# A hybrid attention and Fourier layer on eight cores: the Fourier projection on half the tokens, own keys computed late, side work spread over attention

## The chip, the cores and the metric

The kernel runs on all eight cores of one Trainium2 chip. Each pair of cores has one batch entry of four; each core owns 1024 of its 2048 tokens. Cores exchange nothing. The metric is the device time of the slowest core, in microseconds (us). Some runs are in a second, slower state, in which the cores of one die show a lower granted TensorE clock: in the run of 1853.86 us of the changed kernel cores 0 to 3 had 0.87 and took 1799 to 1852 us, cores 4 to 7 had 0.98 to 0.99 and took 1634 to 1638 us. A ratio is the mean time of one kernel's fast runs over that of the other's of the same rounds on the same chip, so it is not quite the ratio of the medians quoted beside it.

Names: PE is TensorE, ACT ScalarE, DVE VectorE, POOL GpSimd, SP SyncE. "ada blocks" are the 48 column blocks of the weight matrix that makes shift, scale and gate from the conditioning vector (tiles wada, wadm, wadb, by the buffer they land in).

## The reference, cut to what matters

```python
mod = silu(c) @ w_ada + b_ada                  # shift1, scale1, gate1, shift2, scale2, gate2
h = rmsnorm(x, g1) * (1 + scale1) + shift1
q, k, v, u = split(h @ w_in)                   # 1536 | 512 | 512 | 512 columns
q = rope(rmsnorm(q)); k = rope(rmsnorm(k))
attn = softmax(q @ [k_ctx, k].T / sqrt(128)) @ [v_ctx, v]     # 12 heads, 4 key heads, 256 context keys
four = Re(fft2(u over (positions, 128 channels))) @ w_f       # per group of 128 channels
x = x + gate1 * (concat(attn, four) @ w_out)
x = x + gate2 * (relu(modulate(rmsnorm(x, g2), ...) @ w1)**2 @ w2)
return rmsnorm(x, final_g)
```

A core needs keys and values for all 2048 tokens and 256 context tokens, but queries only for its own 1024. For the Fourier part it needs u of all positions.

Of the kernel before, what the change touches and what calls it, by code (L numbers as in the profile page):

```python
# [409 lines left out]
ORDER = [8, 12, 9, 13, 10, 14, 11, 15, 0, 4, 1, 5, 16, 17, 2, 6, 3, 7]  # L410
KORDER = [ORDER[n] for n in (5, 6, 7, 0, 8, 1, 9, 2, 10, 3, 11, 4, 14, 15, 16, 17)]

# [12 lines left out]
def _slots():  # L425
    o = 0
    for n, w in (('ident', 128), ('ones', 128), ('selb', 384), ('sel2', 2), ('dcol', 8)):
        CB[n] = (o, w)
        o += w
    CB['_'] = (o, 0)  # L430
    o = 0
    for n, w in (('g1', 16), ('g2', 16), ('fg', 16), ('bada', 96), ('c', 32), ('qg', 256), ('kg', 256), ('dmask', 1)):
        CF[n] = (o, w)
        o += w
    CF['_'] = (o, 0)
# [5 lines left out]
def build_program():  # L441
# [10 lines left out]
    wvu_d = din("w_vu", [128, 16 * 1024])  # L452
# [8 lines left out]
    ct_d = din("dft_c", [128, 8 * 512])  # L461
    st_d = din("dft_s", [128, 8 * 512])
    rr_d = din("dft_r", [2, 512])
# [3 lines left out]
    with ExitStack() as st:  # L467
# [22 lines left out]
        stat = small('stat', [18, 3])  # L490
# [3 lines left out]
        dsum = small('dsum', [4])  # L494
        dbf = small('dbf', [4], BF16)
# [3 lines left out]
        o_ub = o[0]  # L499
        ub = [small('ub_%d' % i, [512], BF16) for i in range(2)]  # L500
# [7 lines left out]
        ident, ones, sel2 = cbv('ident'), cbv('ones'), cbv('sel2')  # L508
# [7 lines left out]
        WVU = at('wvu', 60, [16, 1024], BF16)  # L516
        WV, WU = WVU[:, :, 0:512], WVU[:, :, 512:1024]
        WK = at('wk', 92, [16, 512], BF16)
        WQ = [at('wq_0', 60, [16, 512], BF16), at('wq_1', 44, [16, 512], BF16)]
        Ue = at('ue', 44, [8, 512], BF16)  # L520
        Uo = at('uo', 52, [8, 512], BF16)
        qT = at('qT', 76, [12, 1024], BF16)
        mixF = at('mixF', 100, [4, 1024], BF16)
# [5 lines left out]
        XS = [at('xs_%d' % i, kb, [16, 128]) for i, kb in enumerate((144, 152, 160, 192))]  # L529
        XI = [0, 1, 2, 3, 0, 1, 2, 0, 1, 2, 0, 1, 0, 1, 0, 1, 0, 1]  # L530
        SQ = [at('sqx_%d' % i, 168 + 4 * i, [16, 128], BF16) for i in range(2)]
        Y = [at('y_%d' % i, 176 + 2 * i, [512]) for i in range(4)]
        YL = Y[0:1] + [at('yl_%d' % i, kb, [512]) for i, kb in enumerate((46, 54, 140, 142, 186, 190))]
# [3 lines left out]
        BR = [at('br_%d' % i, 192 + i, [512], BF16) for i in range(2)]  # L537
        BK, BKC, BVD = [at(n, 194 + 2 * i, [512]) for i, n in enumerate(('bk', 'bkc', 'bvd'))]
        BQ = [at('bq_0', 194, [512]), at('bq_1', 196, [512])]
# [4 lines left out]
        CT = at('dftc', 144, [8, 512], BF16)  # L544
        ST = at('dfts', 152, [8, 512], BF16)
        AB = [at('ab_%d' % i, 160 + i, [512], BF16) for i in range(4)]
        WCS = at('wcs', 164, [3, 4, 128], BF16)
        RR = [at('rr_0', 167, [512], BF16), at('rr_1', 206, [512], BF16)]
        WFT = at('wft', 168, [512])
        CCS = at('ccs', 170, [256])  # L550
# [8 lines left out]
        SQA = R.buf('sqa', o_ub, [512])  # L559
# [27 lines left out]
        R.dma('sp', cf, cf_d[:, :], 'cf')  # L587
        R.dma('pool', cb, cb_d[:, :], 'cb')
# [6 lines left out]
        def ada(i, slots, key, dlevel, level, banks, after=()):  # L595
# [3 lines left out]
            d = R.dma('pool', w.rearrange("p k n -> p (k n)"), rows(wada_d, i), '%s%d' % (key, s), level=dlevel, after=after)  # L599
# [16 lines left out]
        def bias_rows(w, bank, level):  # L616

            R.level = level
            R.mms([(PS[bank][32 * j:32 * j + 32, :], shp[:, q + j, :], w[:, q + j, :], q == 0, q == 12)
                   for q in range(0, 16, 4) for j in range(4)])  # L620
            R.copy(BR[0], PS[bank])
            R.tt(BR[1], PS[bank], BR[0], ALU.subtract)

        def bias_bc(sel, bank, dst):
            R.mms([(PS[bank], sel, BR[0], True, False), (PS[bank], sel, BR[1], False, True)])
            R.copy(dst, PS[bank])
# [12 lines left out]

        last = []  # L640
        for i in range(8):
            last = ada(8 + i, AD0, 'ada', 0.0, 0.0, [7, 6], last)
            last = [R.dma('pool', WVU[:, 2 * i:2 * i + 2, :].rearrange("p k n -> p (k n)"),
                          wvu_d[:, 2048 * i:2048 * (i + 1)], 'wvu_%d' % i, level=0.0, after=last)]
# [54 lines left out]
        HS = [0, 1, 2, 3, 4, 5, 6, 7, 0, 1, 2, 3, 4, 5, 6, 7, 4, 5]  # L699
        hslot = {}  # L700
        NLATE = 7
        ny = 0

        def vu(n):
# [6 lines left out]
            sq = SQ[n % 2]  # L711
            R.act(sq.rearrange("p k n -> p (k n)"), x.rearrange("p k n -> p (k n)"), AF.Square)
            sb = 6 + n % 2 if n < 3 else 5
# [5 lines left out]
            h = H[HS[n]]  # L719
            hslot[t] = (h, rstd)  # L720
            w_ = 2 if n < 3 else 8
            R.level = 0.95
            for q in range(0, 16 if n < 3 else 8, w_):
                R.tt(h[:, q:q + w_, :], x[:, q:q + w_, :],
                     gs[:, q:q + w_, r].unsqueeze(2).to_broadcast([128, w_, 128]), ALU.mult)
            if n >= 3:
# [8 lines left out]
            b = proj(WV, n, 2) if n < 3 else proj(WV, rot('pb', 3))  # L735
# [5 lines left out]
            if r == 0:  # L741
                b = proj(WU, 3 + n, 2) if n < 3 else proj(WU, rot('pb', 3))
                j = (0 if t < 8 else 4) + t % 4
                if t % 8 < 4:
                    R.act(UA, PS[b], AF.Copy, scale=rstd)
                    R.ts(s3[:, 2:3], rstd, -1.0, None, ALU.mult)
                else:
                    R.ts(s3[:, 2:3], rstd, -1.0, None, ALU.mult)
                    R.stt(Ue[:, j, :], PS[b], rstd, UA, ALU.mult, ALU.add)
                    R.stt(Uo[:, j, :], PS[b], s3[:, 2:3], UA, ALU.mult, ALU.add)  # L750
                    if t % 4 == 0:
                        R.act(ub[t // 8][0:1, :], PS[b][0:1, :], AF.Copy, scale=rstd[0:1, :])

            def keys():
                R.level = 1
                b = proj(WK, 3 + (rot('kb', 2) if n < NLATE else 0))
                y = YL[n] if n < NLATE else Y[1 + rot('yk', 3)]
# [17 lines left out]
        first = [vu(n) for n in range(4)]  # L775
        last = load_win(3, WK, 'wk', 0.1, last)
        for i in range(8):
            last = ada(i, AD0[0:2], 'adz', 0.2, 0.5, [7, 6], last)
# [7 lines left out]

        chains = [keys() for keys in first] + [vu(n)() for n in range(4, NLATE)]
        some = [vu(n) for n in range(NLATE, 10)]
        for n in (5, 6):
            chains[n](0)  # L790
        for n in range(NLATE, 18):
            if n >= 15:
                some += [vu(i) for i in range(15, 18) if n == 15]
            (some.pop(0) if some else vu(n))()()
            if n < NLATE + 5:
                chains[n - NLATE]()
            if 10 <= n < 15:
                ada(6 + n, ADM, 'adm', 1, 1, [4], last)


        def q_block(cbk, pbanks, tbanks, tiles=range(8)):
            w = WQ[cbk % 2]
            bq = BQ[cbk % 2]
            if 0 in tiles:
                bias_rows(w, tbanks[rot('tq', len(tbanks))], R.level)
                bias_bc(selb[0], tbanks[rot('tq', len(tbanks))], bq)
            for t in tiles:
                h, rstd = hslot[t]
                b = pbanks[rot('pq', len(pbanks))]
                R.acc(PS[b], [(h[:, k, :], w[:, k, :]) for k in range(16)])  # L810
                yield qk(b, Y[rot('yd', 4)], rstd, bq, RQ[t // 4][:, t % 4, :], qg2, qT[:, cbk * 4:cbk * 4 + 4, t * 128:(t + 1) * 128])

        def load_wq(cbk, level):
            load_win(cbk, WQ[cbk % 2], 'wq%d' % (cbk % 2), level)


# [3 lines left out]
        for i in range(2):  # L820
            R.dma('pool', RR[i][0:1, :], rr_d[i:i + 1, :], 'rr%d' % i)
        for i in range(2):
            R.dma('sp', RQ[i].rearrange("p k n -> p (k n)"), ropeq_d[:, 512 * i:512 * (i + 1)], 'ropeq%d' % i)
# [3 lines left out]
        def mb():  # L827
            return 6 + rot('misc', 2)
        for i in range(2):
# [4 lines left out]
            if i == 1:  # L834
                R.ts(WCS[:, 2, :, :].rearrange("p g d -> p (g d)"), PS[b], -1.0, None, ALU.mult)
        b = mb()
        for g in range(4):
            R.mms([(PS[b][:, g:g + 1], Ue[:, j, g * 128:(g + 1) * 128], cb[:, CB['dcol'][0] + j:CB['dcol'][0] + j + 1], j == 0, j == 7)
                   for j in range(8)])
        R.copy(dsum, PS[b][:, 0:4])  # L840
        for g in range(4):
# [3 lines left out]
            R.acc(PS[b], [(Ue[:, j, gc], CT[:, j, :]) for j in range(8)] + [(ub[i][0:1, gc], RR[i][0:1, :]) for i in range(2)], step=5)  # L845
            R.copy(xb_, PS[b], 'act')
            R.tt(xb_[:, 0:1], PS[b][:, 0:1], buc[:, g:g + 1], ALU.add)
            R.tt(dbf[:, g:g + 1], PS[b][:, 0:1], dsum[:, g:g + 1], ALU.add)
            b = mb()
            R.acc(PS[b], [(Uo[:, j, gc], ST[:, j, :]) for j in range(8)])  # L850
# [5 lines left out]
            R.mms([(PS[b][:, 1:512], WCS[:, 0, g, :], xb_[:, 1:512], True, False),  # L856
# [8 lines left out]
        for out in q_block(0, [0, 1, 2, 3], [5], range(4)):  # L865
            if done:
                done(5)
# [326 lines left out]
```

## The kernel before: the parts that the change touches

A helper records every operation with what it reads and writes. A list scheduler then orders each engine's stream beforehand with modelled durations, by level and program order. Each engine gets its stream in that order, and the traces show it kept: the six cores whose traces hold all matmul records (10687) have them in one and the same order. Because of the helper all matmuls have the same line in the profile, and one goes by tile names.

A token tile n (128 tokens) is scaled into h. V and U projections follow (16 matmuls of 512 columns each), then K. The shift enters later as a bias (tile bk and others), since h W + shift W can be split:

```python
def vu(n):
    ...                                        # x tile loaded, sum of squares, h = x * gs
    b = proj(WV, ...)                          # V
    R.act(V[:, n, :, 0:128], h3(PS[b]), AF.Copy, scale=rstd)
    if r == 0:                                 # all 16 latent tiles
        b = proj(WU, ...)                      # U; tokens i and 2048 - i in paired tiles
        if t % 8 < 4: R.act(UA, PS[b], AF.Copy, scale=rstd)
        else:                                  # even and odd part of the pair
            R.stt(Ue[:, j, :], PS[b], rstd, UA, ALU.mult, ALU.add)
            R.stt(Uo[:, j, :], PS[b], s3[:, 2:3], UA, ALU.mult, ALU.add)
    def keys(): ...                            # K, and link(): bias, norm, rope, transpose into kT
```

The position DFT uses cosines on the even part and sines on the odd part, each over 8 tiles of 128 positions, for 4 channel groups:

```python
R.acc(PS[b], [(Ue[:, j, gc], CT[:, j, :]) for j in range(8)] + [(ub[i][0:1, gc], RR[i][0:1, :]) for i in range(2)], step=5)
R.acc(PS[b], [(Uo[:, j, gc], ST[:, j, :]) for j in range(8)])
```

Attention has 24 units (12 heads, two query halves), each with 18 key chunks: one 512-column score matmul, exp on ACT, four 129-column matmuls with V. Query projections ("side work") and ada blocks are handed out between the chunks.

## Time and profile before

Median 1669.6 us of 4 runs (1669.31 to 1721.56).

| what | number | view |
|---|---|---|
| span of the profiled core | 1668.6 us | page, first line |
| matmul work at full rate | 1538.9 us | my sum, below |
| shift bias bk ready | 199 us | chain of waits |
| first score matmul / last one | 341 / 651 us | timeline |
| longest unbroken piece of the MLP, 3921 matmuls | 842 us, 215 ns each | chain of waits |

"Matmul work at full rate" is a sum over all matmul records of columns / 2.4 GHz + 1.5 ns, at least 27 ns each, a quarter for the 32-column groups (in this trace four of these start within 10 ns, the next four 216 ns after the first). The constants are read from the starts of matmuls in this trace, from 300 us on: those of 512, 256 and 128 columns start 216, 109 and 56 ns apart (medians), which is 0.417 ns a column, or 2.4 GHz. The 1.5 ns come from the mean of 214.7 ns in the MLP. Those of one or two columns start 25 to 27 ns apart. "Lost" below is the length of a stage less this sum in it. This is needed because the busy share of PE says little: a matmul of 512 columns is shown as 379 ns long, while they start 215 ns apart.

Lines of the page, kernel before: the span, busy time and count of each engine, and two rows of slices (one digit per 1/40 of the span, in tenths: granted TensorE clock, and the DMA share):

```profile
span 1668.6 us, 28572 instructions; the slowest of 8 cores (1657.8 to 1668.6 us)
...
PE 1583.4 (95%) x10687; PEld 812.0 (49%) x10687; DVE 699.8 (42%) x1261; ACT 653.2 (39%) x1459; POOL 114.6 (7%) x182
...
PEclk9789999999999999999999999999999999999999
DMA  9999875288677995055253255424542454245206
```

The windows view by stage: length, then per engine busy us and instruction count, then granted clock, DMA share and GB/s. The limits are the end of the V loads, the shift, and the first and last score matmul:

```profile
core 1: us, PE busy (x) PEld busy (x) DVE busy (x) ACT busy (x) POOL busy (x), PEclk, DMA share, GB/s
0.00:98.00 98.00, 43.21 (x372) 18.85 (x372) 14.20 (x47) 12.63 (x18) 12.59 (x39) 0.80 1.00 186
98.00:199.00 101.00, 99.57 (x842) 49.97 (x842) 23.45 (x48) 57.39 (x130) 3.70 (x7) 0.97 0.98 221
199.00:341.00 142.00, 132.67 (x991) 65.53 (x990) 96.05 (x193) 88.60 (x345) 5.97 (x16) 0.98 0.47 97
341.00:560.00 219.00, 216.88 (x2398) 142.43 (x2397) 122.97 (x299) 156.45 (x338) 16.52 (x32) 1.00 0.81 140
560.00:651.00 91.00, 86.57 (x1148) 64.48 (x1146) 18.05 (x73) 81.69 (x165) 3.16 (x6) 0.98 0.90 179
```

In the first 98 us DMA is full (share 1.00) and the clock is low (0.80); afterwards PE is nearly always busy (99, 93, 99 and 95% of the next four rows). In the fifth row ACT is busy 82 of 91 us. PE's waits in the first 100 us of the kernel before, with what ended them (total us, times, longest), then, of the same kernel, four pieces of the chain that ended last (start, us, what):

```profile
PE ps L116 <- DMA wada_77<-w_ada: 23.7, 2, 22.9
PE ps L116 <- DMA wvu<-w_vu: 20.1, 8, 5.0
```

```profile
199.40 0.70 DVE bk L168
...
255.52 16.91 DMA wadm<-w_ada
...
562.30 43.41 DMA wadb_82<-w_ada
...
784.65 841.96 PE ps L116 x3921
```

The waits show that loads set PE's pace at the start. The chain shows where else something other than PE decided: the shift at 199 us, wadm in the key stage, and 43 us of wadb late in attention. Its last large piece is most of the MLP. Two groups of matmuls of the kernel before by form, for later (output and inputs, shapes, count, busy us and mean ns of one, idle time before): 64 V and U matmuls of one buffer, and the cosine half of the DFT:

```profile
L116 PE MATMUL ps<-wvu,h_62 128*128 128x512 bf16 x64 | 14.9, 379 | 0.0
...
L116 PE MATMUL ps<-dftc,ue 128*128 128x512 bf16 x32 | 7.6, 379 | 0.1
```

### The profile page before, as it was taken

To read this page: it belongs to the slowest core of one execution; us is meant where nothing else is said; L and a number is where in the kernel's file an instruction comes from. 1 tells how busy PE (TensorE), PEld (TensorE's weight loads), DVE (VectorE), ACT (ScalarE), POOL (GpSimd) and SP (SyncE) were. 2 spreads that over 40 slices of the span, in tenths; PEclk is the share of its full clock that TensorE was granted. 3 is DMA by queue.
4 is the path that set the end of the run, shared out by engine and by line. 5 is a ranking of instruction groups with operands and counts; after the bars stand their busy time and mean duration, and the time that the engine had idled before them with its cause. 6 is when DMAs were issued, how large, how long until landed. Compare 5 with 4: busy or idle time off the path is not lost.

```text
span 1668.6 us, 28572 instructions; the slowest of 8 cores (1657.8 to 1668.6 us)
## 1 busy us (share of the span) xinstructions
PE 1583.4 (95%) x10687; PEld 812.0 (49%) x10687; DVE 699.8 (42%) x1261; ACT 653.2 (39%) x1459; POOL 114.6 (7%) x182
## 2 busy tenths in 40 slices
PE   1689999999999999999999999999999999999996
PEld 0245544456666666444444444444444444444446
DVE  1122474765555312243444444444444444444236
ACT  1055586457777886145211111111111111111266
POOL 1100000000000000331000000000000000000032
PEclk9789999999999999999999999999999999999999
DMA  9999875288677995055253255424542454245206
GB/s 207 170 204 227 184 167 94 47 128 146 116 133 132 204 172 165 1 101 101 51 101 63 45 95 102 70 45 89 101 76 45 82 102 82 42 79 101 51 1 203
DMA packets 29669, 180.48 MB, mean 108 GB/s; under 512 B 2656, under 2 KB 10080, under 8 KB 13664
## 3 DMA queue, kind: packets, MB, share of 16 engines
q0 software_dynamic: 15472, 140.68, 47.7%
q1 hardware_dynamic: 14064, 37.97, 7.0%
q8 instruction: 89, 1.46, 0.3%
q14 instruction: 44, 0.36, 0.1%
HBM read 310.94 MB, written 8.39 MB: 191 GB/s over the span
## 4 chain that ended last, share of the span: by engine, by line
PE 83%; DMA 12%; ACT 2%; issue 1%; DVE 1%; POOL 0%; another core or an unknown queue 0%; DVEq 0%; ACTq 0%; POOLq 0%; SPq 0%
PE ps L116 83%; DMA wvu<-w_vu 5%; DMA wadb_82<-w_ada 3%; DMA wadm<-w_ada 2%; DMA wada_77<-w_ada 1%; DMA xs_86<-xt 1%; PE ps L128 1%; DMA wq_69<-w_in 1%; ACT h_2_150 L147 0%; ACT sqx_90 L147 0%; ACT h_64 L147 0%; ACT t_0_103 L147 0%; ACT h_63 L147 0%; ACT h_66 L147 0%; ACT sqx_89 L147 0%
## 5 line engine op out<-in xcount | busy, mean ns | idle before, releaser
L155 DVE SCALAR_TENSOR_TENSOR acc_147<-ps,modcol,acc_147 128x512 f32<-128x512 f32 (+2 forms) x288 | 197.4, 691 | 256.0 <-PE ps L116 238.9
L116 PE MATMUL ps<-a_1_160,w_1_158 128*128 128x512 bf16 (+2 forms) x1152 | 240.9, 355 | 0.0
L116 PE MATMUL ps<-a_0_159,w_0_157 128*128 128x512 bf16 (+2 forms) x1152 | 240.9, 355 | 0.0
L155 DVE SCALAR_TENSOR_TENSOR acc_145<-ps,modcol,acc_145 128x512 f32<-128x512 f32 x128 | 96.2, 751 | 176.6 <-PE ps L116 167.2
L116 PEld LDWEIGHTS ps<-a_0_159,w_0_157 128*128 128x128 bf16 x1152 | 108.5, 98 | 114.7
L116 PEld LDWEIGHTS ps<-a_1_160,w_1_158 128*128 128x128 bf16 x1152 | 108.7, 98 | 114.0
L155 DVE SCALAR_TENSOR_TENSOR acc_146<-ps,modcol,acc_146 128x512 f32<-128x512 f32 x128 | 96.2, 751 | 136.8 <-PE ps L116 127.4
L116 PE MATMUL ps<-qT,kT 128*128 128x512 bf16 x432 | 152.0, 380 | 1.0 <-ACT qst L147 0.5
L116 PE MATMUL ps<-h_0_148,w_0_155 128*128 128x512 bf16 x512 | 115.4, 379 | 0.0
L116 PE MATMUL ps<-h_0_148,w_1_156 128*128 128x512 bf16 x512 | 115.2, 379 | 0.0
L116 PE MATMUL ps<-h_2_150,w_0_155 128*128 128x512 bf16 x384 | 88.1, 379 | 0.3 <-ACT h_2_150 L147 0.3
L116 PE MATMUL ps<-h_2_150,w_1_156 128*128 128x512 bf16 x384 | 88.1, 379 | 0.0
L147 ACT ACTIVATE rs_164<-ps 128x512 f32<-128x512 f32 x32 | 19.1, 597 | 162.9 <-PE ps L116 162.9
L147 ACT ACTIVATE rs_161<-ps 128x512 f32<-128x512 f32 x32 | 19.1, 597 | 162.0 <-PE ps L116 162.0
L147 ACT ACTIVATE rs_163<-ps 128x512 f32<-128x512 f32 x32 | 19.1, 596 | 161.7 <-PE ps L116 161.7
L147 ACT ACTIVATE rs_162<-ps 128x512 f32<-128x512 f32 x32 | 19.1, 596 | 160.7 <-PE ps L116 160.7
L116 PEld LDWEIGHTS ps<-h_0_148,w_0_155 128*128 128x128 bf16 x512 | 50.2, 98 | 60.3
L116 PEld LDWEIGHTS ps<-h_0_148,w_1_156 128*128 128x128 bf16 x512 | 50.2, 98 | 60.3
L152 DVE TENSOR_TENSOR modcol<-ps,cf 128x4 f32<-128x4 f32 x48 | 7.6, 159 | 129.3 <-PE ps L116 129.3
L116 PEld LDWEIGHTS ps<-h_2_150,w_0_155 128*128 128x128 bf16 x384 | 37.4, 98 | 46.1 <-issue 1.2
L116 PEld LDWEIGHTS ps<-h_2_150,w_1_156 128*128 128x128 bf16 x384 | 37.5, 98 | 45.3
L116 PEld LDWEIGHTS ps<-qT,kT 128*128 128x128 bf16 x432 | 40.8, 97 | 17.1 <-issue 4.6
(432 smaller groups left out, 2374.1 us busy)
## 6 DMA issues: line engine op xcount, KB each, us to landing
w_0_155<-w POOLq DMA_DIRECT2D x8, 2048.0 KB, 16.1
w_0_157<-w POOLq DMA_DIRECT2D x8, 2048.0 KB, 23.1
w_1_156<-w POOLq DMA_DIRECT2D x8, 2048.0 KB, 16.3
w_1_158<-w POOLq DMA_DIRECT2D x8, 2048.0 KB, 23.1
wadb_82<-w_ada POOLq DMA_DIRECT2D x9, 1024.0 KB, 14.0
wadb_83<-w_ada POOLq DMA_DIRECT2D x9, 1024.0 KB, 14.3
wadb_84<-w_ada POOLq DMA_DIRECT2D x9, 1024.0 KB, 14.5
xs_85<-xt SPq DMA_DIRECT2D x7, 1024.0 KB, 13.4
```

The source lines that it names most:

```text
L116: ins = e.matmul(o, lhsT=l, rhs=r, start=a, stop=b)
L128: ins = e.transpose(out=o, in_=i_, identity=ident)
L147: self.add('act', lambda e: e.activation(out=out, in_=in_, func=func, scale=scale, **kw), reads, writes, dur, level=level)
L152: self.add(eng, lambda e: e.tensor_tensor(out=out, in0=a, in1=b, op=op), [a, b], [out], dur, level=level)
L155: self.add('dve', lambda e: e.scalar_tensor_tensor(out=out, in0=a, scalar=s, in1=b, op0=op0, op1=op1), [a, b] + ([] if isinstance(s, float ...
```

## The change

Its intent has three parts.

1. **Fourier by token parity.** Each core owns the outputs of one parity p. For these, u(k) and u(k + 1024) occur only as u(k) + (-1)^p u(k + 1024). The projection is linear, so the two h tiles are added first, with a per-token factor for the different norms, and only 8 tiles are projected. The position DFT sums over half as many positions.
2. **Own keys late.** h of the core's own eight tiles is kept (for the queries anyway), and their keys are computed once the shift is there, straight into the bias step.
3. **Even side work.** Four query tiles move from before attention into it (20 instead of 16). They, the ada blocks and the output weight loads are spread more evenly.

The core of the diff, with cuts:

```diff
-ORDER = [8, 12, 9, 13, 10, 14, 11, 15, 0, 4, 1, 5, 16, 17, 2, 6, 3, 7]
+ORDER = [8, 14, 10, 12, 9, 15, 11, 13, 0, 6, 2, 4, 1, 7, 3, 5, 16, 17]
+KSEQ = [4, 5, 8, 7, 9, 6, 10, 0, 11, 1, 12, 2, 13, 3, 14, 15, 16, 17]
 ...
+def uprime(n):                                   # for each pair of tiles n-1, n
+    R.act(s3[:, 3:4], s3[:, 0:1], AF.Exp, scale=-0.5, bias=s3[:, 2:3])      # ratio of the norms
+    R.mms([(PS[5][:, 128:256], s3[:, 3:4].to_broadcast([128, 128]), IDF, True, True)])   # to a row, float32
+    for q in (0, 8):
+        R.tt(x[:, q:q + 8, :], hb[:, q:q + 8, :], RHO..., ALU.mult)
+        R.tt(hf[:, q:q + 8, :], ha[:, q:q + 8, :], x[:, q:q + 8, :], ALU.add)
+    R.acc(PS[b], [(hf[:, k, :], WU[:, k, :]) for k in range(16)])
 ...
-        XI = [0, 1, 2, 3, 0, 1, 2, 0, 1, 2, 0, 1, 0, 1, 0, 1, 0, 1]          # x buffers by tile
+        XI = [4, 1, 5, 2, 0, 3, 0, 1, 2, 3, 0, 1, 2, 3, 0, 1, 1, 0]
-        WCS = at('wcs', 164, [3, 4, 128], BF16)
+        WCS = at('wcs', 204, [3, 4, 128], BF16)     # now where RQ[1], the 2nd query rope table, lies
 ...
-    R.acc(PS[b], [(Ue[:, j, gc], CT[:, j, :]) for j in range(8)] + ...
+    R.acc(PS[b], [(Ue[:, j, gc], CT[:, j, :]) for j in range(4)] + [(Uo[0:1, 2 * i, gc], RR[0:1, i, :]) ...
+for m, n in enumerate(KSEQ):
+    if n >= NLATE: links[n] = keys[n]()
+    links[n](0 if n in (4, 5) else None)
+    if 2 <= m < 9: ada(14 + m, ADM, 'adm', 1, 1, [3], last)
 ...
-    q = chain(q_block(1, ...), q_block(2, ...));                       na, nq, done = 21, 0, None
-        while nq < 16 and nq < 1.2 * u:
+    q = chain(q_block(0, ..., range(4, 8)), q_block(1, ...), q_block(2, ...));  na, nq, done = 23, 0, None
+        while nq < 20 and nq < 2 + u:
```

## The prediction

> **What bounds the kernel now.** TensorE (PE). I sum every matmul record at columns / 2.4 GHz + 1.5 ns: 1538.9 us of the 1668.6 us span. The sustained spacing supports that rate: in the chain of waits 3921 matmuls take 841.96 us, 215 ns each[...]. The rest lies, by the same sum, at:
> - 0-100 us: 73 us. DMA share near 1.0 (windows view); PE waits 24 us for wada_77, 20 us for wvu (waits view).
> - 100-200: 3 us, though DMA stays near 1.0; the shift (bias tile bk) is only ready at 199 us.
> - 200-362: 16 us. Keys' norm and rope chains: ACT busy 17 to 19 of 20 us at 200-260; the chain of waits goes through ACT, wadm and wq.
> - 362-656 (attention): 16 us, 12 of them at 560-640, where q side work has run out, ACT has 15 to 19 of 20 us and the chain 43 us of wadb.
> - MLP: nearly full.
>
> **What the change does to PE.**
> - U projections: 16 tiles become 8. 128 matmuls of 512 columns less: -27.5 us.
> - Position DFT: 72 matmuls (8 of them one-row) become 48 (16 of them one-row): -5.2 us.
> - Added: 8 float32 128-column matmuls (281 ns each as traced for wft) and small two-column sums: +2.5 us.
> Net -30 us.
>
> **Other engines.** DVE gains 32 operations of 128x1024 (1.22 us each as traced for h) = +39 us and loses about 12 us, but this falls mostly before 200 us where DVE has only 24 of 102 us busy. Cast traffic is unchanged before the shift (22 MB written at 168 GB/s), so the shift still arrives at 190-200 us. V needs 26 MB instead of 28 MB read first: it finishes near 91 us instead of 98, but the first keys then wait for wk (about 97 and 104 us); I book +3 us. Pre-shift PE work, about 135 us, barely fills PE to 200 us.
> After the shift: 18 key chains, about 3.5 us DVE and 4 us ACT each, against about 103 us of PE work. PE, ACT (about 94) and DVE (about 99) are nearly equal, so I keep 10 to 15 us of loss; attention should start near 312 us instead of 363. It takes four more q tiles (+14.8 us), two ada blocks less (-2), loses about 9 us instead of 16, and ends near 615 us instead of 656. WO loads come later, but their buffers free by about unit 18, 70 us before the end: enough.
>
> **Sum:** 30 on PE, about 3 early, 5 to 7 in attention, less a few us for new chain stalls: -37 us.
>
> **Predicted: 1633 us, range 1619 to 1650.** Faster by over 2% 0.60, within 2% 0.39, slower 0.01.
>
> **Right if:** PE matmul records fall by about 150 net of small ones; attention starts at 305-325 and ends at 605-630; MLP length is unchanged; the 560-640 dip shrinks; bk still appears near 195 us.
> **Wrong step if:** attention starts later than 330 (key chains on ACT/DVE, or single-buffer wadm, now bound the stage); PE idles at 100-190 for x tiles or wk; a gap appears after attention waiting for wo.
>
> **What would make it wrong:** the three engines so evenly loaded at 200-310 us that their waits add up; PE dropping to the lower clock in new idles.

What the trace of the kernel before shows behind its figures: the casting loads moved 168 GB/s as written from 60 to 100 us, with DMA full (share 1.02 to 1.03). One h operation of 128x1024 on DVE took 1.22 us. The 281 ns are the mean length shown for one of the two records of a float32 matmul of 128 columns; they start 112 ns apart. The lower clock named at the end stood beside an idle PE: 0.69 at 35 to 98 us, where PE was busy 38.7 of 63 us, and 0.83 at 260 to 280 us, 16.2 of 20 us; that the idle time brings it about is not shown. The arrival of V, wk and the shift and the times of the key chains are my estimates from such numbers.

## The result

Fast runs of the changed kernel: 1642.43 and 1644.87 us. Two more, 1853.86 and 1846.57 us, are slow (one die at a clock of 0.87), so the median of all four, 1745.7, says nothing. Ratio of the fast runs 0.9845, 95% interval 0.9817 to 0.9874. So it is about 26 us faster, within 2% by the classes used. It lies inside the predicted range, 9 to 12 us above the predicted time. A second set of five rounds on another chip (e_again, below) gave 0.9854.

The same lines of the page of the changed kernel:

```profile
span 1640.9 us, 28405 instructions; the slowest of 8 cores (1627.7 to 1640.9 us)
...
PE 1553.7 (95%) x10567; PEld 799.3 (49%) x10567; DVE 734.7 (45%) x1312; ACT 642.7 (39%) x1446; POOL 118.3 (7%) x189
...
PEclk9899999899999999999999999999999999999998
DMA  9999895577675993084045315532552255235206
```

The windows view of the changed kernel by the same stages, from 98 us on (limits: shift, first and last score matmul):

```profile
core 0: us, PE busy (x) PEld busy (x) DVE busy (x) ACT busy (x) POOL busy (x), PEclk, DMA share, GB/s
...
98.00:219.00 121.00, 115.83 (x950) 58.40 (x950) 63.56 (x93) 72.92 (x177) 8.44 (x16) 0.99 0.96 212
219.00:319.00 100.00, 94.76 (x791) 47.22 (x791) 84.10 (x179) 62.06 (x283) 6.87 (x13) 0.93 0.64 115
319.00:560.00 241.00, 236.61 (x2645) 158.48 (x2643) 121.17 (x308) 180.50 (x386) 13.19 (x25) 0.99 0.72 128
560.00:622.00 62.00, 59.58 (x780) 43.62 (x778) 18.97 (x61) 55.56 (x115) 3.70 (x7) 1.00 0.96 188
```

PE has 120 matmul records fewer. The first score matmul starts at 319 instead of 341 us, the last at 622 instead of 651. But the shift is there at 219, not 199 us. Four pieces of the chain that ended last, changed kernel:

```profile
219.23 0.70 DVE bk L168
...
235.16 16.81 DMA wadm<-w_ada
...
318.02 14.26 DMA ropeq_127<-rope_q
...
574.31 32.41 DMA wadb_88<-w_ada
```

The chain still has wadm and wadb, 20 us of lateness in bk, and a new piece just before attention: ropeq_127, the second query rope table. Its long piece of 3921 matmuls of the MLP takes 841.96 us as before (the whole MLP 891 us in both kernels). The groups by form of the changed kernel:

```profile
L116 PE MATMUL ps<-wu,hf_75 128*128 128x512 bf16 x64 | 15.1, 379 | 0.0
L116 PE MATMUL ps<-wu,hf_74 128*128 128x512 bf16 x64 | 15.1, 379 | 0.0
...
L116 PE MATMUL ps<-dftc,ue 128*128 128x512 bf16 x16 | 4.9, 439 | 0.2 <-ACT mixF L166 0.2
```

The Fourier projection has 128 matmuls in all. Before, it had 256 of the 544 that V and U shared. The cosine half of the DFT has 16 instead of 32, but its mean rose from 379 to 439 ns: four of them ran from 288.9 us on, while the granted clock was 0.50 (287.5 to 297.7 us), and took up to 634 ns each. The 8 float32 broadcasts show as 16 records in the same view.

Because the slowest core's windows vary from core to core, the accounting is best read as the median over the cores. The lost columns use the six cores whose traces hold all matmul records.

| median over cores | before | after | difference |
|---|---|---|---|
| span | 1663.8 | 1634.7 | -29.1 |
| matmul work at full rate | 1538.9 | 1507.5 | -31.4 |
| lost until the shift | 76.0 | 75.8 | -0.2 |
| lost from the shift to the first score matmul | 13.8 | 14.2 | +0.4 |
| lost in attention | 14.5 | 15.7 | +1.2 |
| loss from a lower clock, 200 to 700 us (part of the two rows above) | 3.4 | 7.6 | +4.2 |

So the kernel got faster by the matmul work that was taken out, and by nothing else. Everything that parts 2 and 3 of the change were meant to save in waiting was not saved, or was lost again. The slowest core, which sets the time, gained a little less than the median one: 27.7 us in the profiled runs, 26 us by the mean of the fast runs. The cores lie further apart than before (13.2 us from the fastest to the slowest in the profiled run, instead of 10.8).

### The profile page after: what moved, and what is told of

Same layout as the page of the kernel before. It is cut to its first block, busy times and chain, and to the rows that moved or that the text cites. A ratio compares the mean times of both kernels' runs of the same rounds, so it can differ in the third digit from the quotient of the medians.

```text
span 1640.9 us, 28405 instructions; the slowest of 8 cores (1627.7 to 1640.9 us)
## 1 busy us (share of the span) xinstructions
PE 1553.7 (95%) x10567; PEld 799.3 (49%) x10567; DVE 734.7 (45%) x1312; ACT 642.7 (39%) x1446; POOL 118.3 (7%) x189
## 4 chain that ended last, share of the span: by engine, by line
PE 84%; DMA 9%; ACT 3%; issue 2%; DVE 1%; POOL 0%; DVEq 0%; ACTq 0%; POOLq 0%; SPq 0%
PE ps L116 83%; DMA wada_83<-w_ada 4%; DMA wadb_88<-w_ada 2%; DMA xs_91<-xt 1%; DMA wadm<-w_ada 1%; DMA ropeq_127<-rope_q 1%; PE ps L128 1%; ACT sqx_97 L147 0%; ACT h_2_159 L147 0%; ACT xb_114 L147 0%; DVE xs_91 L152 0%; ACT xb_113 L147 0%; ACT t_0_111 L147 0%; DVE hf_74 L152 0%; ACT t_1_112 L147 0%
## 5 line engine op out<-in xcount | busy, mean ns | idle before, releaser
L116 PE MATMUL ps<-qT_78,kT 128*128 128x512 bf16 x144 | 51.6, 378 | 0.0
L116 PE MATMUL ps<-qT_76,kT 128*128 128x512 bf16 x144 | 50.5, 387 | 0.0
## 6 DMA issues: line engine op xcount, KB each, us to landing
w_0_163<-w POOLq DMA_DIRECT2D x8, 2048.0 KB, 14.7
wadb_87<-w_ada POOLq DMA_DIRECT2D x9, 1024.0 KB, 10.2
```

What stands on the lines that cost most here:

```text
L116: ins = e.matmul(o, lhsT=l, rhs=r, start=a, stop=b)
```

## The experiments

Twelve kernels ran. Every kernel but the two that were made wrong gave the right result.

### e_double_u: is the removed matmul time worth its full length?

```diff
-            R.acc(PS[b], [(hf[:, k, :], WU[:, k, :]) for k in range(16)])
+            for _ in range(2):
+                R.acc(PS[b], [(hf[:, k, :], WU[:, k, :]) for k in range(16)])
```

> The changed kernel with each of the eight combined Fourier projections computed twice (same result): 128 matmuls of 512 columns, 27.5 us of PE, are put back. Theory A (PE is the limit of the stage, so removed matmul time is removed span): fast runs about 1668 to 1672 us, ratio to before 0.998 to 1.002. Rival B (the stage before the shift is paced by loads, so the halved projection mostly opened slack on PE): 1648 to 1658 us, ratio 0.987 to 0.993.

Measured: fast runs 1664.7 to 1673.3 us, ratio 1.0006 (0.9983 to 1.0029). The median span rose from 1634.7 to 1661.1 us, 26.4 us for 27.5 us of matmul work. The first score matmul moved from 314 to 337 us, while bk stayed at 217. The page of e_double_u, span and engines:

```profile
span 1663.0 us, 28663 instructions; the slowest of 8 cores (1658.0 to 1663.0 us)
...
PE 1577.1 (95%) x10695; PEld 811.1 (49%) x10695; DVE 738.2 (44%) x1312; ACT 645.2 (39%) x1446; POOL 118.4 (7%) x189
```

Theory A holds: although loads fill DMA until the shift (share 0.99 to 98 us, 0.94 from there to 217 us in e_double_u), matmul time taken out there comes off the span nearly one for one (26.4 of 27.5 us).

### e_gift, e_rq1_noadm, e_rq1_noadm_gift: what does the late shift cost?

e_gift leaves out the loads of the last four shift blocks:

```diff
-            last = ada(i, AD0[0:2], 'adz', 0.2, 0.5, [7, 6], last, 2)
+            last = ada(i, AD0[0:2], 'adz', 0.2, 0.5, [7, 6], last, 2, i < 4)   # load only the first four
```

> The changed kernel without the loads of the last four shift blocks (their matmuls run on the blocks loaded before; the result is wrong on purpose). The shift should be there some 35 us earlier (bk near 185 instead of 219 us) with the same PE work. Theory C (the late shift costs what the prediction missed, because the key chains start late): 10 to 18 us faster than the changed kernel, near 1627 us, ratio 0.974. Rival D (PE has enough other work until then, the late shift is nearly free): within 4 us of the changed kernel, ratio 0.982 to 0.986.

Measured: 1644.1 to 1646.3 us, ratio 0.986 (0.9845 to 0.9876). bk came at 194 instead of 217 us (median), yet the first score matmul came at 318 instead of 314. By its numbers that is rival D. But the trace shows a new wait where the gain went. The largest wait of PE between the shift and attention in e_gift, and then two issues of wadm loads in the timeline of its POOL queue (start, us, engine; in brackets, idle before and its releaser):

```profile
PE ps L116 <- DMA wadm<-w_ada: 7.4, 1, 7.4
```

```profile
219.64 0.53 POOL L178 DMA_DIRECT2D wadm<-w_ada  x1
247.57 0.53 POOL L178 DMA_DIRECT2D wadm<-w_ada  x1 [27.40 <-PE ps L116]
```

The earlier chains only met a wadm block earlier: its load sat in the queue behind query weights and DFT tables and took 26 us, and PE, which runs in fixed order, stood before its matmuls. The granted clock then fell to 0.50 for 10 to 14 us in all eight cores, from 237 us on (in the profiled core 12 key matmuls of 512 columns took 5.28 us at 246.89 us, another 12 took 2.75 us at 252.39 us). So e_gift alone doesn't decide. The next two kernels take the wadm blocks out of the key stage, on top of e_rq1 (described below):

```diff
-            if 2 <= m < 9:
-                ada(14 + m, ADM, 'adm', 1, 1, [3], last)
-            na, nq, done = 23, 0, None
+            na, nq, done = 16, 0, None
-                while na < 48 and na - 23 < min(1.2 * u, 12 + 1.0 * (u - 10)):
+                while na < 48 and na - 16 < min(1.5 * u, 15 + 1.35 * (u - 10)):
```

> The changed kernel with the second query rope table freed (as in e_rq1) and with the seven ada blocks of the key stage moved into attention (32 ada blocks there). PE work is the same. Theory (the single-buffer wadm loads and their tiny matmuls hold PE in the key stage: the 3 us wait at 249 us, the half clock records at 252 and 285 us): the stage from the shift to attention loses about 8 us instead of 17 to 19, attention starts near 302 us, total 3 to 6 us faster than e_rq1, ratio 0.978 to 0.980. Rival (attention cannot take seven more blocks of weight loads, 6 us of load each): the end of attention waits for wadb and the total is equal to or slower than e_rq1.

Measured: 1646.7 to 1648.7 us, ratio 0.9871 (0.9854 to 0.9888), 10 us slower than e_rq1 instead of faster. The theory fell, and the rival's reason was not what showed either. PE waited for wadb only 1.6 us at the end of attention. The loss was in the key stage: the re-planned order brought bk only at 226 us, and PE waited 5.0 us for the bias rows (DVE br). The stage lost 20.0 us instead of 15.4. It seems that the blocks that were in the way had also been work to do; that is argued, not shown.

> e_rq1_noadm without the loads of the last four shift blocks (wrong on purpose), so that the shift is there about 25 us earlier while no wadm block can stand in the way of PE afterwards, as it did in e_gift (7.4 us wait). Theory C (an early shift is worth 8 us or more once wadm does not eat it): at least 8 us faster than e_rq1_noadm. Rival D (PE is full until the shift anyway and the stage after it is held by the key chains and by PE work): within 3 us of e_rq1_noadm.

Measured: 1636.5 to 1638.7 us, ratio 0.981 (0.9793 to 0.9827): 10 us faster than e_rq1_noadm, so theory C holds for this pair. bk came at 193 instead of 226 us, the first score matmul at 303 instead of 319. But the pair's base had become worse by its own change. Against e_rq1, with the late shift and the wadm blocks, the time is the same (1636.4 to 1638.1, on another chip). The median span is 6 us lower (1625.0 against 1630.8). So 25 us of earlier shift, with 24 us of loads given away (four blocks at about 6 us each by the 168 GB/s of the casting loads), buys at most some 6 us on a middle core and nothing that shows in the slowest one.

### e_rq1: the second query rope table

In the changed kernel the Fourier channel tables WCS lie where the second rope table RQ[1] will be. So that table loads only when the Fourier part has ended. Two lines of the timeline of the changed kernel (columns as above), and its largest wait of PE at 290 to 350 us:

```profile
318.02 0.33 SPq L178 DMA_DIRECT2D ropeq_127<-rope_q  x1
...
332.37 0.43 DVE L152 TENSOR_TENSOR ropeg_128<-ropeq_127,cf 128x256 f32<-128x256 f32 x1 [4.47 <-DMA ropeq_127<-rope_q]
```

```profile
PE ps L128 <- DVE xb_113 L152: 4.4, 1, 4.4
```

The 256 KB load was issued at 318.02 us and took 14.3 us; 4 MB of casting loads (as written) had been issued to POOL's queue just before it (at 314 to 317 us). That these made it so slow is not shown: the first query rope table, of the same size, took 5.2 us at 227.65 us, and DMA was full both times (share 1.03 and 1.04). DVE stood for it 4.5 us with the first side query tile. PE, in order, stood 4.4 us before that tile's transpose (xb_113). The edit puts the three tables into a part of the query buffer that is free until the first queries are written:

```diff
-        WCS = at('wcs', 204, [3, 4, 128], BF16)
+        WCS = [at('wcs_%d' % i, 77 + 2 * i, [4, 128], BF16) for i in range(3)]
```

> The changed kernel with the three Fourier channel tables moved out of the place of the second query rope table, so that this table loads before the Fourier part ends instead of at 318 us, right before attention. Theory: the 4.4 us wait of PE at 332 us and the half-clock stretch after it go, attention loses 10 us instead of 18: 4 to 8 us faster than the changed kernel, ratio about 0.981. Rival: the wait is only moved (the same chains end when they end): within 2 us.

Measured: 1636.4 to 1638.1 us, ratio 0.9814 (0.9798 to 0.9829). The same wait view of e_rq1, core 0, largest wait:

```profile
PE ps L116 <- ACT qT L166: 0.8, 1, 0.8
```

The load is issued at 207 to 225 us, the 4.4 us wait is gone, and attention takes 297.5 instead of 301.8 us (medians). No core has a half-clock record (granted clock 0.50) between 290 and 580 us; in the changed kernel five of eight had one, of 3.4 or 6.8 us, at 328 to 338 us. Attention's loss is 11.5 instead of 15.7 us. This is the fastest correct kernel that ran.

### e_again: how sure is the difference?

The changed kernel unedited, on the chip of the following three.

> The changed kernel itself once more, five rounds on the same chip as the next three, because its first runs held only two fast ones. Theory: ratio 0.983 to 0.987 against before, so that e_rq1 (0.9814) is a true gain of 4 to 6 us. Rival: 0.981 to 0.982, and the gain of e_rq1 was noise between chips.

Measured: ratio 0.9854 (0.9804 to 0.9905). The interval is wide because one of five runs counted as fast took 1661.8 us; the other four took 1639.8 to 1644.3. Attention took 302.0 us again. By time alone e_rq1's gain is not settled: its interval overlaps those of both sets of the changed kernel, and the means of the fast runs, without the 1661.8, differ by 4 to 7 us, on different chips. By the stage it is 4 us, in both pairs.

### e_rq1_ctx, e_rq1_shift2, e_rq1_ctx_fewadm: can the shift be had earlier by order?

```diff
# e_rq1_ctx
-            keys[n] = vu(n)                      # n = 16, 17, the context tiles
+            keys[n] = vu(n, last)                # meant: x loaded after the last shift block
# e_rq1_shift2: two shift blocks before the weights of U
+        for i in range(2):
+            last = ada(i, AD0[0:2], 'adz', 0.1, 0.5, [7, 6], last, 2)
         for q in range(4):
             last = load_quarter(WU, wu_d, q, 'wu', 0.1, last)
# e_rq1_ctx_fewadm: three wadm blocks in the key stage
-            if 2 <= m < 9:
-                ada(14 + m, ADM, 'adm', 1, 1, [3], last)
+            if m in (5, 9, 13):
+                ada(16 + (m - 5) // 4, ADM, 'adm', 1, 1, [3], last)
```

> e_rq1 with the x loads of the two context tiles issued only after the last shift block, so that they do not take DMA time from it (2 MB, about 6 us). Theory (the shift comes late because the tiles' loads share the DMA engines with the shift blocks, and it is on the critical path): bk 4 to 7 us earlier, 2 to 4 us faster than e_rq1. Rival (the shift's arrival does not matter within a few us, or the context tiles then come late themselves): within 1.5 us of e_rq1.

> e_rq1 with the first two shift blocks loaded before the Fourier projection weights instead of after them. Theory (an earlier shift is worth its time, as e_rq1_noadm_gift against e_rq1_noadm had it, 10 us for 32 us earlier): bk about 10 us earlier, 2 to 4 us faster than e_rq1. Rival (the projections that wait for those weights are then late and PE idles before the shift): equal or up to 5 us slower.

> e_rq1_ctx with three of the seven wadm blocks left in the key stage and four moved to attention. Theory (with fewer single-buffer blocks PE waits less for wadm, and attention can load four more): 2 to 4 us faster than e_rq1_ctx. Rival (as e_rq1_noadm: the stage had the blocks' matmuls as filler and the schedule without them is worse): slower by up to 8 us.

The 6 us for 2 MB of x in the first of these are an estimate from the traces: from 98 us to the shift the packets of the x queue took about 3 us of all 16 engines' time per MB (3.1 before, 3.0 in the changed kernel).

Measured: e_rq1_ctx 0.9820 (0.9795 to 0.9846), bk at 221 us; e_rq1_shift2 0.9850 (0.9825 to 0.9875), bk at 219 us; e_rq1_ctx_fewadm 0.9821 (0.9798 to 0.9843), bk at 222 us. None moved bk to an earlier time, so none tests what an earlier shift is worth. Nor do they show what sets it. The edit of e_rq1_ctx did not take effect as meant: `after` orders only the scheduler's plan, no semaphore holds the SP queue to it, and the last two x loads were issued at 182 and 195 us (medians), as in e_rq1. The last shift block landed at 205 us (207 in e_rq1), but the re-planned order put its matmuls behind those of a context tile, and they ran 11 us after the landing instead of 4. In e_rq1_shift2 the first two shift blocks were issued some 20 us earlier, yet the last one landed at 205 us too.

All three lost 5 to 6 us more before the shift (80.8, 82.0 and 81.1 against 75.5 us). For e_rq1_shift2 that is the size of its rival, but its reason is not shown: PE's waits from 90 to 222 us name no load of U weights on any core.

### e_spread: tiny matmuls and the clock

In the changed kernel every core has half-clock records in the key stage, six of eight at 282 to 290 us. Two windows of about the length of one such record, slowest core, changed kernel (columns as in the windows views above):

```profile
core 0: us, PE busy (x) PEld busy (x) DVE busy (x) ACT busy (x) POOL busy (x), PEclk, DMA share, GB/s
...
284.10:287.50 3.40, 3.40 (x55) 2.64 (x53) 2.45 (x5) 2.50 (x13) 0.00 (x0) 0.99 0.16 34
287.50:290.90 3.40, 3.40 (x42) 1.86 (x41) 2.76 (x8) 2.62 (x9) 0.53 (x1) 0.50 0.16 17
```

At 284.1 to 287.5 us PE is busy all of the 3.4 us with 55 matmuls, most of them two columns wide, worth 2.2 us at full rate. In the next window the granted clock is 0.50. The edit puts the 48 two-column sums into the four DFT groups:

```diff
-        for g in range(4): R.mms([... 12 two-column matmuls of group g ...])      # in one run
+            (the same 12 at the end of each pass of the group loop, own copy)
```

> The changed kernel with the 48 two-column Fourier sums put into the four groups of the DFT instead of in one run before it. Theory (the run of tiny matmuls at 283 to 288 us lets the clock fall to half for 3 to 10 us in every core): no clock record of 0.5 near 285 us, 2 to 5 us faster, ratio about 0.982. Rival (clock falls for the idle time between groups, not for the tiny ones): half-clock record stays and the time is within 1.5 us of the changed kernel.

Measured: ratio 0.992 (0.9827 to 1.0012), inconclusive. In the profiled run four cores had a mean granted clock of 0.965 to 0.970, the others 0.984 to 0.988; it was 0.81 in those four for long stretches between 262 and 425 us, and two of the three runs counted as fast took 1666 us. The four undisturbed cores took 1637.6 to 1642.1 us, the same cores of the changed kernel 1627.7 to 1640.9. In these four the record near 285 us is gone, but two of them have one of 10.2 us at 302 instead. So the drop moved; no gain is shown. That the tiny matmuls cause it is argued, not shown; nor is the idle time of the rival.

### e_even_only and e_uneven: the third part by itself, and undone

e_even_only puts the new hand-out of side work (20 query tiles in attention, ada blocks from 21 on) into the kernel before:

```diff
-            q = chain(q_block(1, [6, 7], [7, 6]), q_block(2, [6, 7], [7, 6]))
+            q = chain(q_block(0, [6, 7], [7, 6], range(4, 8)), q_block(1, [6, 7], [7, 6]), q_block(2, [6, 7], [7, 6]))
-                while nq < 16 and nq < 1.2 * u:
+                while nq < 20 and nq < 2 + u:
```

> The kernel before with only the third part of the change: 20 query tiles spread over 18 units of attention and ada blocks paced after them. PE work is the same as before. Theory (even side work by itself is worth what the end of attention lost): 5 to 8 us faster than before, ratio 0.995 to 0.997. Rival (no gain without the other parts, because attention then starts no earlier by as much as it grows): ratio 0.999 to 1.001.

Measured: ratio 0.999 (0.996 to 1.002). No gain in time. On the median core attention lost 11.3 instead of 14.5 us and the span fell by 4 us; in the slowest core it did not come through. So the part is worth 3 to 4 us on a middle core, about half of what I had expected.

e_uneven is the changed kernel with this part undone (the same lines the other way round, ada blocks from 23).

> The changed kernel with the third part undone: the four remaining query tiles of the first block are computed before attention again, and queries and ada blocks are handed out in attention as in the kernel before (16 query tiles, 1.2 per unit, used up by unit 14). PE work is the same. Theory (the even side work pays because the last units have exp on ACT as their limit when no side work is left): attention's end part fills worse, 5 to 9 us slower than the changed kernel, ratio 0.988 to 0.991 against before. Rival (the four tiles cost more at the start of attention, where they wait for the late query rope table, than they give at the end): the same or faster, ratio 0.980 to 0.985.

Measured: 1647.1 to 1651.0 us, ratio 0.9884 (0.9864 to 0.9903), so 6 us slower than the changed kernel, as the theory's number said. The place is another one, though. The profiled core fills the last part of attention as well as the changed kernel does (PE busy 78.1 against 77.6 of 80 us at 560 to 640 us). It loses at 330 to 340 us, where the late rope table again holds PE (3.7 us of waiting for xb), and at 380 to 390 us, where it waits for wadb (1.9 us). Attention lost 23.8 us. The size was right and the reason was not shown. Nor does this run isolate the hand-out at the end: it also puts the four query tiles before attention again.

## Why the prediction was right, and where its sum was off

The time lay in the range, and the gain was 26 us instead of 37. That put it within 2%, to which I had given 0.39, and not above 2%, to which I had given 0.60. One term carries the result, the matmul work; the terms for waiting did not come, and the range was wide enough for that. Point by point:

- **Matmul work: right.** I said -30 us; the sum over records fell by 31.4 us, and e_double_u showed that it comes off the span nearly one for one (26.4 of 27.5 us). Records fell by 120, not 150: small matmuls and two records for each float32 matmul.
- **"The shift still arrives at 190-200 us": wrong.** bk came at 217 us (median). I had counted the cast traffic, and that was right; I had left out the x loads that share the DMA engines with it (from 98 us to the shift, in the profiled cores, the cast packets took 64% of the engines' time and those of the queue of x 34% before, 63% and 33% now). Packets summed by queue, until the last shift block landed (medians): 23.5 MB cast and 14.7 MB of x by 188.0 us before, 23.3 MB cast and 19.7 MB of x by 207.5 us now. At the 207 GB/s that both queues together moved until then, 5 MB more of x are 24 us by my estimate; 19.5 us were seen. The x loads come earlier because all V and U projections now precede the shift, and more x buffers let them. The last blocks also came one by one through two buffers. No run tests this, since none of the edits of the order took the x loads away, so the cause is argued from the sums. It cost little: PE had other work, and the loss until the shift stayed at 76 us.
- **"+3 us early": wrong.** The loss until the shift did not change.
- **"Attention should start near 312 us instead of 363": the step was mis-measured.** By the first score matmul, attention started at 339 before and 314 after (medians). For the kernel before I had taken 363 us, where the score matmuls become dense, and for the changed one the start. The stage gave 25 us, not 51, and with it none of the waiting. That 314 is so near 312 is two errors that cancel: the shift came 18 us later than before, but only 83 us of PE work were left between it and attention, not 103. PE had done 142 us before the shift, not 135, and the two together are 13 us less than I had counted.
- **"Loses about 9 us instead of 16" in attention: wrong, and the largest part of the missing 11 us.** It lost 15.7 us. e_rq1 shows 4 us of this: the second rope table, placed where the Fourier tables lie, came after the Fourier part. I had listed the buffers of weights and x tiles and not this one. The even hand-out of side work by itself gave 3 us of the 7 that I had booked. The dip at 560 to 640 us shrank as said, from 7 to 5 us lost on the median core; the loss moved to the start of attention, with 4.3 us at 320 to 340 us.
- **PE dropping to the lower clock, named under what would make it wrong, did happen:** 7.6 us instead of 3.4 by 700 us in the median. It goes with the spread between the cores: between 220 and 345 us core 0 (1640.9 us) had 20 us at half clock, core 1 (1627.7 us) 7 us.
- **"Equally loaded at 200-310 us": the size was right.** The stage lost 14.2 us, within the 10 to 15 I had kept. That equal load is the reason is not shown: the chain goes through bk and a wadm load there.
- **No gap for wo after attention: right.** Less than 1 us was lost between the last score matmul and the MLP.

Of the clock itself the records of the two kernels show this: between 200 and 700 us every drop is to 0.50 and lasts 3.4, 6.8 or 10.2 us, but for one spell of 0.81 in each of two cores of the changed kernel (7.8 us at 320 us).

## What to carry to other kernels

Where PE is busy nearly all the time, count the matmul columns that a change takes out and expect that much (here PE was busy 95% of the span, and 31.4 us less of matmul work made the median span 29.1 us shorter); book nothing for waits that it is "also" meant to remove until each has been traced to the load or the buffer that ends it. When a change moves a buffer, list every later tile that shares its place: here a 256 KB table behind a 3 KB-per-partition neighbour cost 4 us of attention, and moving the neighbour gave the fastest correct kernel. When an edit of order is meant to test something, look first whether the loads were in fact issued in the new order. When an upper bound experiment (a load given away) shows no gain, look where the gain went before calling the cause harmless, because in a fixed order the next late load can stand in its place, as wadm did for 7.4 us in e_gift.

## What else the traces showed of the hardware

- In the traces of both kernels all eight cores ran the MLP at a granted clock of 1.00 (680 to 1640 us before, 660 to 1620 us after; PE busy 954 to 960 of 960 us), 215 ns per 512 columns. 0.81 appeared only in spells (7.8 us at 320 us in two cores; long stretches in four cores of e_spread). In the slow runs the mean clock of a die's cores was down to 0.83 to 0.84 (e_spread, 1887 us); no trace of one was kept, so the cause is not shown.
- The clock fell to 0.50 after PE had stood (changed kernel, slowest core: PE busy 2.3 of 5.3 us at 330.0 to 335.3 us, then 6.8 us at 0.50). It also fell after a 3.4 us window that the records show as fully busy with PE work, 55 matmuls worth 2.2 us of columns (the profile models the ends of matmuls, so short idle times may hide in that). What makes it fall is not shown.
- Each float32 matmul of 128 columns is two records, 112 ns apart, together about four times the 53 ns that 128 columns take at the 2.4 GHz read above (bf16 ones start 56 ns apart).
- Loads that cast float32 to bf16, with nothing beside them: the kernel before moved 168 GB/s as written, at a DMA share of 1.02 (60 to 80 us); the changed one 3.4 MB per 20 us, 171 GB/s, at the same place.
